# A decoder layer on one core: rsqrt on VectorE, a home for wo's last weights, queries stored in reading order, a third output tile

## Chip, cores and metric

The kernel runs on one core of one Trainium2 chip. The metric is the device time of one execution in microseconds (us). The core has five engines that run side by side, each through its own instructions in order: TensorE (PE, matmuls and transposes), VectorE (DVE), ScalarE (ACT), GpSimd (POOL) and SyncE (SP, which here issues nearly all DMAs).

## The reference, cut to what matters

```python
def hybrid_mixer(u, pos, w_in, g_cq, g_ckv, w_uq, w_uk, w_uv, w_iq, w_up_a, w_up_b, w_o):
    ...
    o_a = dsa_branch(c_q, c_kv, k_rope, k_idx, w_idx, pos, w_uq, w_uk, w_uv, w_iq)
    o_b = dilated_branch(qkv_b.reshape(B, S, 3, N_GROUPS_B, H_B, D_HEAD_B), pos)
    g_a, g_b = jnp.split(gates, 2, axis=-1)
    z = jax.nn.sigmoid(g_a) * (o_a @ w_up_a) + jax.nn.sigmoid(g_b) * (o_b @ w_up_b)
    return z @ w_o

def reference(x, c, positions, ...):
    ...
    h = rms_norm(x, g_pre_ffn1) * (1 + sc1) + sh1
    x = x + 0.5 * gt1 * rms_norm(swiglu(h, w_gate1, w_up1, w_down1), g_post_ffn1)
    u = rms_norm(x, g_pre_mix) * (1 + sc2) + sh2
    y = hybrid_mixer(u, positions, ...)
    x = x + gt2 * rms_norm(y, g_post_mix)
    h = rms_norm(x, g_pre_ffn2) * (1 + sc3) + sh3
    return x + 0.5 * gt3 * rms_norm(swiglu(h, w_gate2, w_up2, w_down2), g_post_ffn2)
```

There are 1024 tokens, a model width of 1024 and a hidden width of 2816, all in float32. Branch A is a sparse attention: each token's index scores choose 256 earlier keys (top-k), and eight heads attend to these. Branch B is a dilated sliding window with three groups (g = 0, 1, 2) of four heads.

## The kernel before

A float32 matmul is made of three passes over operands that are split into a high and a low part (`mm3`, lines 104 to 106; the split is a copy on ACT, L76, and a subtraction on DVE, L77, or on POOL, L82). The tokens are eight tiles t of 128. The order in which instructions stand on each engine is set when the program is built, by a scheduler that lists what is ready by its own cost estimates; tile pools with a fixed number of buffers are part of what it looks at. On the chip every engine then runs its list in order and waits on semaphores.

In time the program goes: modulation and the first feed-forward (to about 757 us), `mixer_front` (the projections of u, the index scores and branch A's queries), `branch_b`, `branch_a`, `mixer_out`, the output projection `wo`, and the second feed-forward (FFN2).

**Queries.** `mixer_front` makes branch A's queries for one token tile at a time as a high part `qh` and a low part `ql` of 128 x 8 x 128 numbers, and stores each in DRAM as one block of `qd` (L823, L824). `branch_a` works on head pairs p. Its `queries(p)` (L1158) loads the two heads of a pair, high and low, for all eight tiles into `QQ` (the trace's `aq`): four DMAs of 512 KB each per pair, sixteen in all.

**Branch B.** For each group there are eight steps T of 128 queries. A step projects q, k (`bq`) and, for g = 0, v (`bv`); DVE applies the rotation (L994, L996); PE transposes to `bqT`, `KH` and `KL` (L1015); PE makes scores `bs` for two heads (L1033, L1034); DVE adds the mask and takes the maximum (L1037, which also writes columns of `ob`); ACT exponentiates (L1042); PE transposes (`bpt`, L1048) and multiplies with the values `bV` (L1056, L1059); ACT and DVE put the result in `ob` (L1063, L1064); and SP stores `ob` to `bd` (L1069). The tile `ob` has two buffers. For g = 1 and 2 the values are loaded from `vd` (L988). The first group's weights come in through raw buffers `wbr` (L944) of the pool `r3`, three of them. The gates' projections `gpj`, whose weights `gr` are loaded on L903, and the top-k's counting rounds on DVE (L849) run at the same time as the first group.

**Branch A's start.** It loads keys `KK`, `Ke`, `Ko` (L1119) and the queries, makes `kpj`, then scores `as`. Later `combine_b` reads `bd` back (`br`, L1076).

**wo.** The loop is over two halves h of four token tiles and two column halves c. One set of weights (one h, one c) is eight row blocks of 128 x 512, each with a high tile (`woh`) and a low tile (`wol`), in a pool `w3` of thirteen buffers. For each of the four token tiles j, `wo` is summed over eight k, three passes each. After both column halves, `residual` and `prenorm` follow for each tile. Each contains one `rsqrt`: eight small instructions on numbers of 128 x 1 (L88, L89, then three rounds of L94 and L95), and L1292 ahead of the first. They run on POOL, except the residual of t = 4, 6 and the prenorm of t = 5, 7, which run on DVE. The large steps L1294 (residual) and L1302 (prenorm) are on DVE. `xt` holds the residual stream of a half; the first half's is in the tile `gab`, the second half's in the third buffer of the tag `z`, whose first two hold `mixer_out`'s result.

**FFN2's start.** `first_half` turns (L208, L214) and splits the first half's normed rows to the operands V[0] and V[1]; `second_half` needs the second half's rows too and makes differences of the two (L232 on DVE) for V[2] to V[6]. `gate_up` prepares combined weights on POOL (L286 to L289) and runs the matmuls `gu`; DVE and POOL combine what comes out (L372, L380).

Of the kernel before, what the change touches and what calls it, by code (L numbers as in the profile page):

```python
# [10 lines left out]
F32 = mybir.dt.float32  # L11
F32R = mybir.dt.float32r
# [8 lines left out]
D = 1024  # L21
S = 1024
DFF = 2816
P = 128
# [11 lines left out]
def f(t):  # L36
    return t.bitcast(F32)


class Layer:  # L40
# [581 lines left out]
        nc.vector.tensor_tensor(out1, out1, t[0], op=ALU.subtract)  # L622
        nc.vector.tensor_tensor(out2, out2, t[1], op=ALU.add)

    def load_w(self, W, src, n, name, rows=1024, per=None, split=None, rawp=None):

        nc = self.nc
        per = per or 1024 // n
        his, los = [], []
        nk = rows // P  # L630
        for k0 in range(0, nk, per):
            m = min(per, nk - k0)
            r = (rawp or self.rawp).tile([P, m, n], F32, name=f"{name}r", tag="raw")
            nc.sync.dma_start(r, src[k0 * P:(k0 + m) * P, :].rearrange("(k p) f -> p k f", p=P))
            for j in range(m):
                hi = W.tile([P, n], F32R, name=f"{name}h", tag="w")
                lo = W.tile([P, n], F32R, name=f"{name}l", tag="w")
                (split or self.split)(hi, lo, r[:, j, :])
                his.append(hi)
                los.append(lo)  # L640
        return his, los

    def mixer_front(self, uT, second, W, cp, ce, mk, tb):
# [150 lines left out]
        for t in range(8):  # L794
# [22 lines left out]
            for g in range(2):  # L817
                bt = self.bank("qtr")
                for j in range(4):
                    nc.tensor.transpose(bt[:, j * P:(j + 1) * P], qt[:, 4 * g + j, :], self.ident)  # L820
                self.split(qh[:, 4 * g:4 * g + 4, :].rearrange("p a b -> p (a b)"),
                           ql[:, 4 * g:4 * g + 4, :].rearrange("p a b -> p (a b)"), bt)
            nc.sync.dma_start(self.qd[0, t], f(qh))  # L823
            nc.sync.dma_start(self.qd[1, t], f(ql))  # L824
        return sc, gp, idxp

    def topk(self, sc, pool, mask, off, bp):
# [85 lines left out]
    def branch_b(self, uT, W, bp, last, gates, raws):  # L913
# [9 lines left out]
        for g in (0, None, 1, 2):  # L923
# [37 lines left out]
            for T in range(8):  # L961
# [61 lines left out]
                else:  # L1023
                    blocks, lo_c, kk = [(0, V), (1, prev)], 0, lambda x: x[:, 0::2, :]
                Pm = [bp.tile([P, 2, 256], F32, name="bP", tag="bP", bufs=2) for _ in range(2)]
                ob = bp.tile([P, 264], F32, name="ob", bufs=2)
                mask = self.wide[g // 2][:, P:] if prev is not None and slot == 0 else self.wide[g // 2]
                for hp in range(2):
                    bs = self.bank("bs", tag="s")
# [69 lines left out]
    def branch_a(self, aw, ap, late, G, mask, off):  # L1099
# [55 lines left out]
        def queries(p):  # L1155
            for e in range(2):
                for l in range(2):
                    nc.sync.dma_start(f(QQ[:, e, l]), self.qd[l, :, :, 2 * p + e, :].rearrange("t p q -> p t q"))  # L1158

        keys(0)  # L1160
        queries(0)
# [145 lines left out]
def layer_kernel(ctx, tc, aps, out):  # L1307
    nc = tc.nc
# [108 lines left out]
    with pool("mk") as mk:  # L1417
        mask = mk.tile([P, o], BF, name="mask")
        L.turns = {}
        with pool("cp") as cp, pool("wa", 16) as W, pool("ce") as ce, pool("r2", 4) as L.rawp, pool("tb") as tb:  # L1420
            def second():
                L.emit_hT(uT, 1, [y1[:, j, :] for j in range(4)], sh2)
                right.close()
                ixp = ix.enter_context(pool("ix", side="right"))
                return right.enter_context(pool("gp", side="right")), ixp

            sc, gp, ixp = L.mixer_front(uT, second, W, cp, ce, mk, tb)
        with pool("wb", 24) as W, pool("bp") as bp, pool("r3", 3) as L.rawp:
            def raws():
                right.close()  # L1430
                return right.enter_context(pool("r7", 3, side="right"))

            L.branch_b(uT, W, bp, lambda: L.topk(sc, ixp, mask, off, bp), lambda: L.gates(uT, gp), raws)
            L.turns = {}
        right.close()
        ix.close()
        gq = right.enter_context(pool("gq", side="right"))
        G = gq.tile([P, 4096], F32R, name="gbuf")
        with pool("r4", 2, side="right") as L.rawp, pool("aw", side="right") as aw, pool("ap") as ap, pool("al") as late:
            oA, oB, wa0 = L.branch_a(aw, ap, late, G, mask, off)  # L1440
# [3 lines left out]
    with pool("w3", 13) as W, pool("r5", 3) as L.rawp, pool("o2") as op:  # L1444
# [5 lines left out]
        with pool("zp") as zp:  # L1450
# [6 lines left out]
            ss = sums()  # L1457
            for h in range(2):
                ys[h] = L.big.tile([P, 4, D], F32, name=f"wy{h}", tag="big")
                xt = zp.tile([P, 4, D], F32, name=f"xt{h}", **(dict(tag="z", bufs=3) if h else dict(tag="gab")))  # L1460
                nc.sync.dma_start(xt, L.x1[4 * h * P:(4 * h + 4) * P, :].rearrange("(t p) d -> p t d", p=P))
                for c in range(2):
                    cl = slice(c * 512, (c + 1) * 512)
                    wh, wl = L.load_w(W, aps["w_o"][0][:, cl], 512, "wo")
                    for j in range(4):
                        b = L.bank("wo", tag="pj")
                        for k in range(8):
                            L.mm3(b, z[h][0][:, k, tok(j)], z[h][1][:, k, tok(j)], wh[k], wl[k], k == 0, k == 7)
                        L.evac(jk, b, ys[h][:, j, cl], G[:, cl], ss[4 * h + j][:, c:c + 1])
                for j in range(4):  # L1470
                    t = 4 * h + j
                    L.residual(ys[h][:, j, :], xt[:, j, :], ss[t], ss[t][:, 2:3], nc.vector if t in (4, 6) else nc.gpsimd)
                    nc.sync.dma_start(x2[tok(t), :], xt[:, j, :])
                    L.prenorm(ys[h][:, j, :], xt[:, j, :], None, ss[t][:, 2:3], ss[t][:, 3:4], nc.vector if t in (5, 7) else nc.gpsimd)
                if h == 0:
                    V[0], V[1] = bigv(0), bigv(1)
                    L.first_half(V, ys[0], range(8), sh, a3)
# [69 lines left out]
```

## Time and profile before

| | before |
|---|---|
| median of 3 runs | 2488.96 us (2488.2 to 2491.31) |
| profiled execution, its own time | 2492.64 us |
| span of that execution in the trace | 2490.9 us |
| mean granted TensorE clock, as a share of full speed | 0.971 |
| PE busy | 2333.2 us (94%) |
| DVE busy | 1664.0 us (67%) |
| ACT busy | 1091.1 us (44%) |
| POOL busy | 1002.8 us (40%) |
| mean rate of the DMA queues | 132 GB/s |

Times in rows are us from the start of the span. A busy PE is one whose matmuls run or stand in the pipeline. Where a row says that an engine was idle "<-X", X is the instruction that released it by the trace. A granted clock of 1.00 is 2.4 GHz, and 0.50 is 1.2 GHz.

### The profile page before, as it was taken

How to read it: one execution, taken by the hardware profiler on the slowest of the kernel's cores; microseconds unless marked ns; L12 is line 12 of the kernel's file. 1: busy time of each engine (PE TensorE's matmuls, PEld its weight loads, DVE VectorE, ACT ScalarE, POOL GpSimd, SP SyncE). 2: the span in 40 equal slices, each digit the busy share in tenths (PEclk: the TensorE clock that was granted, in tenths of full speed). 3: DMA queues.
4: the chain of work that ended last, by engine and by line, in shares of the span. 5: the costliest groups of instructions: out<-in, count | busy, mean ns of one | idle time of the engine just before them, and what ended most of it. 6: DMA issues, size and time to landing. Idle time of an engine off the chain costs nothing.

```text
span 2490.9 us, 33864 instructions
## 1 busy us (share of the span) xinstructions
PE 2333.2 (94%) x11211; PEld 1956.6 (79%) x11211; DVE 1664.0 (67%) x3236; ACT 1091.1 (44%) x2346; POOL 1002.8 (40%) x1122
## 2 busy tenths in 40 slices
PE   5799999989998999999989799889889999999997
PEld 4588877778887977888989688768667888887876
DVE  7865779753886135899973378864477656555786
ACT  5432223323454345677635567632453333233443
POOL 5675555400004433242244200300488756652533
PEclk9899999999999999999999899999989999999999
DMA  9334554671543233521422422143343333336755
GB/s 280 92 103 127 150 156 147 222 268 51 182 137 107 78 100 99 177 63 35 131 85 59 108 69 69 52 169 127 127 135 117 126 108 111 94 123 232 245 194 203
DMA packets 244171, 327.55 MB, mean 132 GB/s; under 512 B 24535, under 2 KB 145271, under 8 KB 243997
## 3 DMA queue, kind: packets, MB, share of 16 engines
q1 hardware_dynamic: 243356, 324.33, 40.8%
q8 instruction: 89, 1.46, 0.2%
q10 hardware_dynamic: 640, 1.07, 0.1%
q14 instruction: 86, 0.70, 0.1%
HBM read 252.07 MB, written 73.27 MB: 131 GB/s over the span
## 4 chain that ended last, share of the span: by engine, by line
PE 69%; DVE 14%; DMA 7%; issue 4%; POOL 4%; ACT 3%; SPq 0%; DVEq 0%; POOLq 0%; ACTq 0%
PE gu L105 9%; PE gu L104 9%; PE gu L106 9%; PE dn L106 4%; PE dn L105 4%; PE dn L104 4%; PE gpj L104 2%; DMA wr<-in_w_mod_dram 2%; PE gpj L105 2%; PE gpj L106 2%; PE bq L104 2%; PE bq L105 2%; PE bq L106 1%; DMA re<-in_w_down_dram 1%; DVE wl L77 1%
## 5 line engine op out<-in xcount | busy, mean ns | idle before, releaser
L104 PE MATMUL gu<-V,wh 128*128 128x512 f32 x1232 | 489.6, 398 | 17.2 <-ACT wh L76 9.3
L105 PE MATMUL gu<-V,wl 128*128 128x512 f32 x1232 | 488.9, 397 | 6.6 <-DVE wl L77 5.7
L106 PE MATMUL gu<-V,wh 128*128 128x512 f32 x1232 | 484.3, 396 | 4.5 <-DVE V L77 4.5
L77 DVE TENSOR_TENSOR wl<-rw,wh 128x512 fp32r<-128x512 f32 x232 | 218.2, 943 | 111.3 <-PE gu L105 80.1
L104 PEld LDWEIGHTS gu<-V,wh 128*128 128x128 f32 x1232 | 235.4, 191 | 71.5 <-ACT wh L76 9.8
L105 PEld LDWEIGHTS gu<-V,wl 128*128 128x128 f32 x1232 | 235.0, 191 | 62.0 <-DVE wl L77 10.4
L106 PEld LDWEIGHTS gu<-V,wh 128*128 128x128 f32 x1232 | 234.6, 191 | 57.2 <-DVE V L77 7.7
L105 PE MATMUL dn<-dh,al 128*128 128x512 f32 x660 | 256.9, 392 | 0.2 <-DVE al L77 0.2
L106 PE MATMUL dn<-dl,ah 128*128 128x512 f32 x660 | 255.2, 392 | 1.1 <-DVE dl L77 1.0
L104 PE MATMUL dn<-dh,ah 128*128 128x512 f32 x660 | 239.0, 392 | 9.1 <-DVE junk L197 6.4
L76 ACT CAST wh<-rw 128x512 fp32r<-128x512 f32 x232 | 139.9, 618 | 213.1 <-PE gu L106 127.7
L372 DVE TENSOR_TENSOR p<-gu,p 128x512 f32<-128x512 f32 x252 | 169.8, 681 | 67.0 <-PE gu L106 33.6
L380 POOL TENSOR_TENSOR p<-p 128x512 f32<-128x512 f32 x86 | 132.1, 1537 | 202.9 <-DVE p L372 73.1
L104 PEld LDWEIGHTS dn<-dh,ah 128*128 128x128 f32 x660 | 124.3, 189 | 35.9 <-DVE junk L197 6.8
L378 ACT ACTIVATE p<-p 128x512 f32<-128x512 f32 x86 | 54.4, 633 | 222.2 <-DVE p L372 173.1
L106 PEld LDWEIGHTS dn<-dl,ah 128*128 128x128 f32 x660 | 124.6, 189 | 28.4 <-DVE dl L77 2.7
L105 PEld LDWEIGHTS dn<-dh,al 128*128 128x128 f32 x660 | 124.5, 189 | 27.3 <-DVE al L77 1.3
L185 DVE SCALAR_TENSOR_TENSOR macc<-wr,scol,macc 128x512 f32<-128x512 f32 x98 | 94.3, 962 | 52.7 <-DMA wr<-in_w_mod_dram 52.0
L76 ACT CAST dh<-rd 128x512 fp32r<-128x512 f32 x110 | 67.9, 619 | 117.5 <-PE dn L105 75.6
L77 DVE TENSOR_TENSOR dl<-rd,dh 128x512 fp32r<-128x512 f32 x110 | 77.1, 704 | 52.2 <-ACT dh L76 48.9
L104 PE MATMUL gpj<-uh,gw 128*128 128x512 f32 x256 | 103.8, 406 | 7.5 <-ACT gt L910 7.3
L849 DVE TENSOR_SCALAR_CACHE_REDUCE mask<-isc,cand 128x384 bf16<-128x384 f32 (+1 forms) x124 | 108.7, 877 | 2.6
(479 smaller groups left out, 5610.7 us busy)
## 6 DMA issues: line engine op xcount, KB each, us to landing
act<-p SPq DMA_DIRECT2D x122, 256.0 KB
rd<-in_w_down_dram SPq DMA_DIRECT2D x58, 512.0 KB
wr<-in_w_mod_dram SPq DMA_DIRECT2D x112, 256.0 KB
rw<-in_w_gate_dram SPq DMA_DIRECT2D x44, 512.0 KB
rw<-in_w_up_dram SPq DMA_DIRECT2D x44, 512.0 KB
ra<-act SPq DMA_DIRECT2D x35, 512.0 KB
act<-act SPq DMA_DIRECT2D x44, 256.0 KB
re<-in_w_down_dram SPq DMA_DIRECT2D x20, 512.0 KB
```

The costliest lines, as they stand in the source:

```text
L76: self.nc.scalar.copy(hi, src)
L77: self.nc.vector.tensor_sub(lo, src, f(hi))
L104: mm(out, ah, bh, start=start, stop=False)
L105: mm(out, al, bh, start=False, stop=False)
L106: mm(out, ah, bl, start=False, stop=stop)
L185: nc.vector.scalar_tensor_tensor(acc, r, self.scol[:, k:k + 1], acc, op0=ALU.mult, op1=ALU.add)
L372: nc.vector.tensor_tensor(x[m], bk, y[m], op=ALU.add)
L378: nc.scalar.activation(x[0], x[0], AF.Silu)
L380: nc.gpsimd.tensor_tensor(x[1], x[1], x[0], op=ALU.mult)
L849: nc.vector.tensor_scalar(mask[:, :(t + 1) * P], sc[t], 0.0 if v is None else one(f(v), t), 0.0, op0=op, op1=ALU.add, accum_out=one(cnt, t))
```

## The change

There are five edits.

1. In `wo`, all `rsqrt` chains and L1292 of `residual` and `prenorm` run on DVE.
2. The last set of `wo` (h = 1, c = 1) keeps its eight high tiles in one tile `wohi` in the third buffer of the tag `z`; only its eight low tiles use the pool `w3`. `xt` of the second half is now in `gab`, after the first half's.
3. `qd` is laid out in the order in which `branch_a` reads it. A store now writes 1024 pieces of 512 B in place of 128 of 4 KB, and a load reads 128 pieces of 4 KB in place of 1024 of 512 B.
4. `ob` has three buffers.
5. The raw pool `r3` of branch B has two buffers.

```diff
@@ load_w
-    def load_w(self, W, src, n, name, rows=1024, per=None, split=None, rawp=None):
+    def load_w(self, W, src, n, name, rows=1024, per=None, split=None, rawp=None, hi=None):
...
-        per = per or 1024 // n
+        per, room = per or 1024 // n, hi
...
-                hi = W.tile([P, n], F32R, name=f"{name}h", tag="w")
+                hi = W.tile([P, n], F32R, name=f"{name}h", tag="w") if room is None else room[:, k0 + j]
@@ mixer_front
-            nc.sync.dma_start(self.qd[0, t], f(qh))
-            nc.sync.dma_start(self.qd[1, t], f(ql))
+            for l, x in enumerate((qh, ql)):
+                nc.sync.dma_start(self.qd[l, :, :, t, :].rearrange("e p q -> p e q"), f(x))
@@ branch_b
-                ob = bp.tile([P, 264], F32, name="ob", bufs=2)
+                ob = bp.tile([P, 264], F32, name="ob", bufs=3)
@@ branch_a, queries
-                    nc.sync.dma_start(f(QQ[:, e, l]), self.qd[l, :, :, 2 * p + e, :].rearrange("t p q -> p t q"))
+                    nc.sync.dma_start(f(QQ[:, e, l]), self.qd[l, 2 * p + e])
@@ the stage of branch B
-        with pool("wb", 24) as W, pool("bp") as bp, pool("r3", 3) as L.rawp:
+        with pool("wb", 24) as W, pool("bp") as bp, pool("r3", 2) as L.rawp:
@@ wo
-                xt = zp.tile([P, 4, D], F32, name=f"xt{h}", **(dict(tag="z", bufs=3) if h else dict(tag="gab")))
+                xt = zp.tile([P, 4, D], F32, name=f"xt{h}", tag="gab")
...
-                    wh, wl = L.load_w(W, aps["w_o"][0][:, cl], 512, "wo")
+                    room = zp.tile([P, 8, 512], F32R, name="wohi", tag="z", bufs=3) if h and c else None
+                    wh, wl = L.load_w(W, aps["w_o"][0][:, cl], 512, "wo", hi=room)
...
-                    L.residual(ys[h][:, j, :], xt[:, j, :], ss[t], ss[t][:, 2:3], nc.vector if t in (4, 6) else nc.gpsimd)
+                    L.residual(ys[h][:, j, :], xt[:, j, :], ss[t], ss[t][:, 2:3], nc.vector)
...
-                    L.prenorm(ys[h][:, j, :], xt[:, j, :], None, ss[t][:, 2:3], ss[t][:, 3:4], nc.vector if t in (5, 7) else nc.gpsimd)
+                    L.prenorm(ys[h][:, j, :], xt[:, j, :], None, ss[t][:, 2:3], ss[t][:, 3:4], nc.vector)
```

The edits move instructions, since the scheduler lists anew. Three places show it.

SP's queue at the end of branch B's last group (T = 0 to 7 of g = 2), where A's keys (`KK`, `Ke`, `Ko`) and queries (`aq`) are loaded among B's stores (`bd<-ob`). Before:

```order
L1069 DMA bd<-ob 128x264
L977 DMA bcs<-csd 128x96
L1119 DMA KK<-krd 64x2x1024 x2
L1158 DMA aq<-qd 128x8x128 x4
L1119 DMA Ke_13582<-krd 64x2x1024
L1119 DMA Ko_13583<-krd 64x2x1024
L988 DMA bV<-vd 128x512 x2
L1069 DMA bd<-ob 128x264 x2
```

And after:

```order
L1119 DMA KK<-krd 64x2x1024 x2
L1158 DMA aq<-qd 128x1024
L977 DMA bcs<-csd 128x96
L988 DMA bV<-vd 128x512 x2
L1069 DMA bd<-ob 128x264
L1158 DMA aq<-qd 128x1024 x3
L1119 DMA Ke_13582<-krd 64x2x1024
L1069 DMA bd<-ob 128x264
L1119 DMA Ko_13583<-krd 64x2x1024
L988 DMA bV<-vd 128x512 x2
L1069 DMA bd<-ob 128x264 x2
```

T=0's store stands ahead of the keys in both. Before, the stores of T=1 and T=2 stood together behind all four query loads; now T=1's stands behind one of them, and T=2's behind the other three and `Ke`.

DVE at the end of `wo`, second half: L398 takes a finished block of `wo` out of PSUM, then the norm of a token tile follows. Before, behind the third and fourth block:

```order
L398 TENSOR_TENSOR wy_16989<-wo,G_16505 128x512
L1292 TENSOR_TENSOR sums<-sums 128x1
L94 TENSOR_SCALAR rs_t<-rs_y,rs_v 128x1
L77 TENSOR_TENSOR wl_17580<-re_17577,wh_17579 128x512
L398 TENSOR_TENSOR wy_16989<-wo,G_16505 128x512
L88 TENSOR_SCALAR rs_v<-sums 128x1
L95 TENSOR_SCALAR rs_y<-rs_t,rs_y 128x1
L89 TENSOR_SCALAR rs_y<-rs_v 128x1
L94 TENSOR_SCALAR rs_t<-rs_y,rs_v 128x1 x2
L95 TENSOR_SCALAR sums<-rs_t,rs_y 128x1
L1294 SCALAR_TENSOR_TENSOR xt_16990<-wy_16989,sums,xt_16990 128x1024
```

After, behind the second block:

```order
L95 TENSOR_SCALAR sums<-rs_t,rs_y 128x1 x2
L1294 SCALAR_TENSOR_TENSOR xt_16990<-wy_16989,sums,xt_16990 128x1024
L1302 TENSOR_SCALAR wy_16989<-xt_16990,sums 128x1024
L398 TENSOR_TENSOR wy_16989<-wo,G_16505 128x512
L1292 TENSOR_TENSOR sums<-sums 128x1
L77 TENSOR_TENSOR wl_17520<-re_17517,wh_17519 128x512
L88 TENSOR_SCALAR rs_v<-sums 128x1 x2
L89 TENSOR_SCALAR rs_y<-rs_v 128x1 x2
L77 TENSOR_TENSOR wl_17526<-re_17523,wh_17525 128x512
L94 TENSOR_SCALAR rs_t<-rs_y,rs_v 128x1 x2
```

Before, the first residual L1294 came after all four evacuations; now a tile's L1294 and the one before's L1302 stand between two evacuations, and a residual's and a prenorm's chains alternate (x2). On PE the last set's matmuls run as four blocks of 24, one token tile after the other, where before each token tile had 18 of them in a first round and its last six (two of the eight k) in a second.

DVE at the start of branch B's first group, where the top-k's counting rounds (L849) stand around the first step's rotation (L994, L996; `bV` is that step's values). Before:

```order
L849 TENSOR_SCALAR mask,cnt<-isc_7463,cand 128x384
L849 TENSOR_SCALAR mask,cnt<-isc_7532,cand 128x512
L849 TENSOR_SCALAR mask,cnt<-isc_7702,cand 128x768
L994 TENSOR_TENSOR qk<-bq,bcs 128x512
L996 TENSOR_TENSOR brt<-bq,bcs 128x512
L866 TENSOR_TENSOR need<-cnt,thr 128x2
L849 TENSOR_SCALAR mask,cnt<-isc_7803,cand 128x896
L77 TENSOR_TENSOR bV<-bv,bV 128x4x64
```

After:

```order
L866 TENSOR_TENSOR need<-cnt,thr 128x2
L849 TENSOR_SCALAR mask,cnt<-isc_7803,cand 128x896
L867 TENSOR_SCALAR acc<-need 128x2
L863 TENSOR_SCALAR acc<-cnt 128x4
L994 TENSOR_TENSOR qk<-bq,bcs 128x512
L996 TENSOR_TENSOR brt<-bq,bcs 128x512
L868 TENSOR_TENSOR pb<-pb,acc 128x2
L864 TENSOR_TENSOR pb<-pb,acc 128x4
L858 TENSOR_SCALAR cand<-pb 128x2
L77 TENSOR_TENSOR bV<-bv,bV 128x4x64
```

In the whole list, 37 of the L849 stood ahead of the first L994, and now 46. PE's gate matmuls `gpj` ahead of the second step's `bq` are 740 of 768, where they were 693.

## Rows read from the trace of the kernel before

**Rows 1.** The page, busy us, share of the span and instructions of each engine

```profile
PE 2333.2 (94%) x11211; PEld 1956.6 (79%) x11211; DVE 1664.0 (67%) x3236; ACT 1091.1 (44%) x2346; POOL 1002.8 (40%) x1122
```

**Rows 2.** Stretches: length; PE, PEld, DVE, ACT, POOL busy (instructions); PE clock; DMA share; GB/s

```profile
1100.00:1250.00 150.00, 149.95 (x878) 138.99 (x876) 142.08 (x447) 102.20 (x239) 38.52 (x43) 1.00 0.26 79
...
1395.40:1451.70 56.30, 38.97 (x229) 33.74 (x227) 20.49 (x65) 28.76 (x83) 8.06 (x9) 0.73 0.38 94
...
1404.60:1421.70 17.10, 7.92 (x39) 7.11 (x39) 4.99 (x20) 6.88 (x22) 4.62 (x5) 0.50 0.37 86
```

**Rows 3.** Chain of waits, end of branch B: start, us, what

```profile
1403.04 10.20 DMA bd<-ob
1413.38 0.42 DVE bP L1037
...
1424.27 2.81 DMA bd<-ob
1427.22 0.43 DVE bP L1037
...
1437.85 2.13 DMA bd<-ob
```

**Rows 4.** SyncE's DMA queue there: start, us, engine, line, what, count

```profile
1390.03 9.32 SPq L1158 DMA_DIRECT2D aq<-qd  x4
...
1403.04 0.86 SPq L1069 DMA_DIRECT2D bd<-ob  x2
```

**Rows 5.** VectorE, end of wo: start, us, instruction, [idle before it <- releaser]

```profile
1779.05 0.75 DVE L1302 TENSOR_SCALAR wy<-xt,sums 128x1024 f32<-128x1024 f32 x1 [0.45 <-POOL sums L95]
...
1804.50 0.69 DVE L77 TENSOR_TENSOR wol<-wor,woh 128x512 fp32r<-128x512 f32 x1 [11.06 <-PE wo L105]
...
1840.31 0.76 DVE L1302 TENSOR_SCALAR wy<-xt,sums 128x1024 f32<-128x1024 f32 x1
...
1843.18 0.95 DVE L232 TENSOR_TENSOR wy<-wy,wy 128x512 f32<-128x512 f32 x1 [1.51 <-ACT wy L216]
```

**Rows 6.** Stretches behind wo's last matmul, columns as in rows 2

```profile
1811.80:1843.20 31.40, 28.94 (x124) 23.27 (x123) 22.53 (x56) 17.55 (x34) 24.51 (x41) 0.95 0.67 217
1843.20:1884.60 41.40, 31.00 (x104) 21.68 (x102) 35.84 (x34) 18.03 (x31) 37.48 (x23) 0.73 0.15 45
1855.20:1872.30 17.10, 13.29 (x34) 9.22 (x35) 17.10 (x18) 9.89 (x18) 13.82 (x9) 0.50 0.25 70
1879.00:1885.80 6.80, 5.89 (x13) 3.68 (x14) 5.59 (x6) 1.24 (x2) 6.17 (x5) 0.50 0.06 9
```

**Rows 7.** VectorE, end of branch B, columns as in rows 5

```profile
1398.62 0.42 DVE L1064 TENSOR_TENSOR ob<-bo,ob 128x256 f32<-128x256 f32 x1 [3.44 <-ACT ob L1063]
```

**Rows 8.** DMA rate in 40 slices, of 1391 to 1399.5 and of 992.6 to 1056 us

```profile
GB/s 366 405 308 289 270 135 212 270 96 251 270 231 135 289 251 135 231 231 96 200 200 193 171 164 224 292 296 299 299 297 296 299 282 296 289 289 292 287 289 292
...
GB/s 206 403 62 10 165 0 0 225 331 194 122 43 0 207 406 293 14 0 10 251 406 5 0 184 395 248 0 85 81 163 406 176 189 237 241 362 254 39 343 277
```

**Rows 9.** Line L94, the whole span: ns min/median/max, first and last start

```profile
L94 DVE TENSOR_SCALAR rs_t<-rs_y,rs_v x63: 253/266/274, 697.6 to 2485.2; 128x1 f32<-128x1 f32 x63
L94 POOL TENSOR_SCALAR rs_t<-rs_y,rs_v x57: 334/341/1820, 1751.5 to 2482.9; 128x1 f32<-128x1 f32 x57
```

**Rows 10.** POOL's groups, 1749 to 1779 us: count | busy us, mean ns | idle before

```profile
L94 POOL TENSOR_SCALAR rs_t<-rs_y,rs_v 128x1 f32<-128x1 f32 x24 | 11.1, 470 | 0.8
```

**Rows 11.** The page's costliest groups, columns as in rows 10

```profile
L849 DVE TENSOR_SCALAR_CACHE_REDUCE mask<-isc,cand 128x384 bf16<-128x384 f32 (+1 forms) x124 | 108.7, 877 | 2.6
```

**Rows 12.** PE's waits, 1030 to 1300 us: us in total, times, longest

```profile
PE bq L104 <- DVE brt L996: 6.5, 3, 3.2
```

**Rows 13.** VectorE's groups, 1843 to 1885 us, columns as in rows 10

```profile
L232 DVE TENSOR_TENSOR wy<-wy,wy 128x512 f32<-128x512 f32 x8 | 10.3, 1285 | 2.7 <-ACT wy L216 1.5 <-POOL V L82 1.2
```

**Rows 14.** VectorE, second half's operands, columns as in rows 5

```profile
1868.03 0.68 DVE L232 TENSOR_TENSOR wy<-wy 128x512 f32<-128x512 f32 x1
...
1875.43 1.76 DVE L232 TENSOR_TENSOR wy<-wy,wy 128x512 f32<-128x512 f32 x1 [1.19 <-POOL V L82]
```

## The prediction

> **What bounds the kernel now.** The page's first line is read first: TensorE (PE) is busy 94% of the span [rows 1]. An edit therefore pays only where PE stands still or has been granted the low clock. The table of stretches says where: from 1100 to 1250 us, with branch B's first group, the gates and the top-k side by side, PE is busy 149.95 of 150 us at clock 1.00, with VectorE (DVE) at 142 [rows 2]. Two other stretches have room, and the change touches both.
>
> The first is the end of branch B's last group. From 1395.4 to 1451.7 us PE works 38.97 of 56.3 us at a mean clock of 0.73 [rows 2]. The chain of waits names the cause [rows 3]: three pieces "DMA bd<-ob" of 10.20, 2.81 and 2.13 us, each ending in DVE's L1037. A step T may write its `ob` only when the store of step T-2 has landed. The store of T=1 is late because of SyncE's queue [rows 4]: the four loads of A's queries hold SP for 9.32 us from 1390.03, and the two `bd` stores behind them leave at 1403.04.
>
> The second is the end of `w_o` and the start of the second feed-forward (FFN2). The last `wo` matmul ends at about 1811.8. DVE stands idle 11.06 us before 1804.50, since the last weight tiles have no slot until PE frees one; the last prenorm L1302 starts at 1840.31, and the second half of V's operands (L232) at 1843.18 [rows 5]. From there to 1884.6 PE works 31.0 of 41.4 us at a mean clock of 0.73, beside a DVE that is busy 35.84 and a GpSimd (POOL) that is busy 37.48 [rows 6].
>
> **Part 1: three ob tiles.** With three tiles, step T waits for the store of T-3. T=3, the one that waited 10.20 us, now waits for T=0's store, which stands ahead of the query loads in SP's order. Its L1037 could go as soon as PE's scores are there, about 1402, not at 1413.38: 11.4 us. T=5 and T=7 then need the stores of T=2 and T=4. In the changed order T=2's store stands behind three query loads and the `Ke` load, 2 MB. At the 297 GB/s that the late slices of the load stretch show [rows 8] they take 7 us; they follow T=1's store, whose `ob` is finished at 1399 [rows 7], so T=2's store lands near 1410 with its own 2 to 3 us. T=5 followed T=3 by 13.84 us before [rows 3], of which 2.81 are a store's wait; so 11 us, and T=5 stands at about 1413, behind that landing. Its wait falls away, and T=7's 2.13 with it: 15.1 us for the three pieces. On top comes clock: PE ran at 0.50 from 1404.6 to 1421.7, with 7.92 us busy [rows 2]; at the full level half of that, 4 us, would go, and I take 3. Sum **-18**. Ends: the whole idle time, 17.3, plus 4 is the most, -21; if T=5 waits for T=2's store as long as T=3 does now, little more than the two small pieces is left, -5.
>
> **Part 2: wo's last set and its norms.** Before, the sixteen tiles of the last set have thirteen slots, so PE runs all four row blocks on six of the eight k first, and every block ends in the last 7 us. With the eight high tiles in `room` the blocks run one after the other: DVE's order now has an evacuation, a norm, an evacuation, a norm. The norms of t=4 to 6 then lie beside the remaining blocks, and only t=7's is left behind the last matmul. Its chain on DVE is the evacuation 0.69, two rsqrt chains of eight small ops (about 1.7 us each, with L94 at 266 ns the longest of them [rows 9]), L1294 1.3 to 2.3 and L1302 0.75: some 8 us with ScalarE's square, and about 14 with the L77 and L372 that stand between. So the last L1302 moves from 28.5 us behind the last `wo` matmul to 14. As DVE sets the pace of the 41.4 us that follow (35.84 busy), what it starts 14 to 16 us earlier ends so much earlier; PE meanwhile has 144 `gu` matmuls that need none of it, 34 us at the 28.94 us for 124 instructions of [rows 6], and transposes. I take -16. The most is what PE could get back from 1811.8 to 1884.6: idle 2.5 and 10.4, and half of the 13.29 and 5.89 us that it works at 0.50 [rows 6], 9.6; together -22. The least, -4, is under the second rival.
>
> The first half's norms (t=0 to 3) now run on DVE too. POOL's 24 L94 took 470 ns each there [rows 10], against DVE's 266 [rows 9]. But DVE must also split some nine weight tiles in that place, and its own sum (eight chains of 1.7, four L1294 of 1.2, four L1302 of 0.7, the splits) is some 28 us from 1750, where the last of these L1302 starts at 1779.05 before [rows 5]. So -2, between 0 and -5. The whole of part 2: **-18**.
>
> POOL's L94 takes 341 ns as a median of all its places [rows 9], and 470 in this one, beside DVE's L1294 [rows 10]. The Trainium skill, "SBUF — State Buffer", section "SBUF: two separate sides", says that VectorE with two SBUF inputs and GpSimd lock each other out for a whole instruction. The rows agree; by it the moved chains lose the stretch, while the L232 that follow stay exposed to POOL.
>
> **Part 3: the queries in DRAM.** The 16 stores of 512 KB now go out in 512 B pieces, and the 16 loads come in whole 4 KB rows. The stores' stretch reaches 406 GB/s in single slices, the loads' 297 [rows 8]. At these, 8.4 MB cost 20.7 or 28.2 us of queue time: +7.5 us, spread over the 64 us in which the stores go out, with idle slices between, so it is hidden unless a `wbr` or `gr` load behind a store is late. Four loads cost 7.1 us before and 5.2 now; in branch A they are hidden save for the `br` reads behind them: -1, between 0 and -3.
>
> The Trainium skill, "DMA: Bandwidth & Descriptors", section "Specifications", gives 512 B as the size from which a transfer runs at line rate. By that neither direction changes, part 3 is 0, and the sum is a microsecond smaller. The rows speak against it (297 against 406 GB/s), though one is a read and the other a write.
>
> **Part 4: B's raw buffers, three to two.** The first group's weights now have two raw tiles. In the changed order nine more of the top-k's counts stand ahead of step T=0's L994; at 877 ns [rows 11] that is 7.9 us. The gates' matmuls move ahead to fill PE, so nothing is lost at once; but they are used up by T=3 rather than T=7, and PE then hangs on DVE, which has 8 us to spare in 150 [rows 2]. Before, PE waits 6.5 us for L996 from 1030 to 1300 [rows 12]. So 0 to +8; I take **+2**, since DVE's work is the same in sum.
>
> **The sum.** -18 - 18 - 1 + 2 = -35. The profiled execution took 2492.64 us: 2457.6. The median, 2488.96, is 3.7 below it, so the forecast is **2454**. By the ends it is 2489 - 21 - 27 - 3 = 2438 to 2489 - 5 - 4 + 8 = 2488.
>
> **Rivals.** First, in B the wait only changes its name: `bV` of T=5 and T=6 and T=2's store all stand behind the query loads, and if those run late T=5 waits as T=3 did. Part 1 gives -6: 2466. For it: SP's queue is the cause now, and one more tile doesn't shorten it. Against: T=5 needs its store 11 us after T=3 starts, and the loads take 7.
>
> Second, FFN2's start is paced by DVE and POOL together. L232 takes a mean of 1285 ns there [rows 13], 0.68 us at the least and 1.76 beside POOL [rows 14]. If the operands come sooner but meet POOL every time, some 24 such ops (L232, V's and the weights' L77) cost 0.5 us more each, 12 us, and part 2 is -6: 2466. The load of `xt` for the second half, now in the tile that the first half frees, can be late in the same place and has the same price. For it: POOL is 91% busy there. Against: the same DVE ops stand beside the same POOL work as before. The first page named above states the lock that would do this.
>
> Third, slower: the first group starves. With two raw tiles each `wbr` load waits for a split that stands behind the top-k in its engine's order, and SP, which issues in order, holds the gates' loads and the 512 B stores back meanwhile. PE then has neither gates nor queries. It decides from 35 us of new PE idle time on; with six counts more of waiting ahead of each of the eight steps, 8 x 6 x 0.877 = 42 us, and 4 us of stores in front, it gives 2500. Against: PE has no idle time in 150 us, and the gates are filler that was moved ahead.
>
> Fourth, the change doesn't do what it says: the stores in B are late for another reason, and the norms wait for the last weights as before. Then only parts 3 and 4 remain: 2490, within 0.2%.
>
> **Chances.** Forecast (2442 to 2462) 0.56; first rival 0.14; second 0.18; third 0.06; fourth 0.06. The range that leaves at most two in ten out reaches from 2438, the sum of the best ends, to 2473, where one part fails in full and the first group costs its 8. A measurement of this kernel can tell 0.2%, 5 us, from no change. Faster 0.88, the same 0.06, slower 0.06.
>
> **What would show it.** In the changed profile the chain in B has no "bd<-ob" piece over 3 us, and the stretch from the query loads to A's first `kpj` is 18 us shorter. From the end of `wo` the last prenorm is about 14 us away, and PE's low clock behind it is gone or short. POOL shows no rsqrt ops in `wo`. The prediction is wrong if L1037 of T=5 waits as T=3 did, if PE stands idle behind `wo` as long as before, or if PE waits over 15 us in all between 1050 and 1300.

## The result and the profile after

| | before | changed |
|---|---|---|
| median | 2488.58 us (2484.29 to 2491.31, 4 runs) | 2470.53 us (2467.49 to 2472.95, 4 runs) |
| ratio to before, 95% interval | | 0.9921 [0.9905, 0.9937] |
| profiled execution; its span | 2492.64; 2490.9 us | 2467.49; 2465.7 us |
| mean granted clock | 0.971 | 0.978 |

The change gains 18 us, where 35 were forecast. The two profiled executions lie 25 us apart, of which 5 arose before the first instruction that the change touches.

To see where the time went, PE's matmuls are counted: every kernel of this study has 11211. Parts of branch B and of `wo` come in another order in some kernels, but at each border below all of them have run the same matmuls, so the start of the n-th can be set against the start of the n-th of before. The table shows what each stage added (+) or saved (-) against the one trace of before, in us. "First" is matmuls 4500 to 6104 (branch B's first group and most of the second), "B's end" 6104 to 6750 (the rest of B and branch A's start), "A" 6750 to 8000 (branch A and the merge), "wo" 8000 to 8750 (from wo to steady FFN2). The stage ahead, of which the change touches only the stores of the queries, shows how far two executions drift. The expectations below count the first stage to matmul 6250, where the kernels with edit 5 still owe 18 of the projections `bq` that before has run; by that border 3 us less are lost and 3 us less are gained (+9.5 and -13.0 for the changed kernel).

Where PE's time is split below, "idle" is time in which PE has no matmul, and "work at 0.50" is time in which it works at the low level, half of which is lost.

| kernel | ahead | first | B's end | A | wo | whole trace |
|---|---|---|---|---|---|---|
| changed | -5.0 | +12.6 | -16.2 | -3.0 | -13.7 | -25.5 |
| changed, once more (e12) | +1.3 | +11.8 | -15.6 | -2.8 | -13.4 | -19.1 |
| e1: two raw buffers | -0.7 | +12.6 | -7.2 | -2.3 | +2.4 | +4.2 |
| e2: queries' layout | +3.1 | -0.3 | -0.3 | -4.0 | +0.1 | -2.1 |
| e3: third ob, two raw buffers | -1.1 | +11.2 | -12.2 | +0.6 | +1.4 | -1.8 |
| e4: both wo edits | -3.7 | +0.4 | +4.8 | -4.3 | -14.3 | -17.1 |
| e5: rsqrt on DVE | -1.5 | +0.4 | +4.8 | -2.1 | -9.2 | -8.7 |
| e6: room for the weights | -3.2 | +0.3 | +5.2 | -3.9 | -8.4 | -10.6 |
| e7: small tile for statistics | -2.2 | -1.8 | -11.1 | -0.6 | -0.8 | -16.9 |
| e8: small tile, queries, wo | -1.2 | +0.6 | -9.9 | -2.7 | -13.2 | -27.4 |
| e11: e8 once more | -2.2 | -1.1 | -11.0 | -3.9 | -14.2 | -31.9 |
| e9: query loads by ACT | -3.4 | +0.1 | +0.8 | -0.5 | 0.0 | -4.2 |
| e10: e8 and query loads by ACT | -2.6 | +0.7 | -13.6 | -2.9 | -13.9 | -32.8 |

Both traces of the changed kernel say the same of each stage within 1 us: a loss of about 12 in the first stage, gains of about 16 in B's end and 13.5 around `wo`, some 3 in between.

**B's first group.** The stretch from 1120 to 1260 us of the changed kernel (columns as in [rows 2]), and PE's waits from 1100 to 1260:

```profile
1120.00:1260.00 140.00, 133.99 (x747) 124.21 (x745) 129.49 (x373) 86.70 (x199) 34.41 (x34) 0.95 0.26 80
```

```profile
PE bo L1056 <- ACT bPT L76: 1.9, 3, 1.2
PE bo L1059 <- DVE bPT L77: 1.5, 2, 1.2
PE bq L104 <- DVE bV L77: 0.9, 1, 0.9
```

Where PE was busy without a break [rows 2], it now stands 6 of 140 us, in waits of 1.2 us and less, and the clock falls to 0.50 twice behind them:

```profile
1183.00:1189.00 6.00, 5.70 (x27) 5.41 (x27) 6.00 (x13) 4.56 (x14) 2.98 (x4) 0.50 0.38 95
1203.20:1209.80 6.60, 6.60 (x24) 5.91 (x25) 6.46 (x22) 4.26 (x11) 0.00 (x0) 0.50 0.28 102
```

The 6 us of idle time and half of these 12.6 us make 12.3, near the table's 12.6. All of the loss lies in the first group: at matmul 5514, which stands at 1230 us in the trace of before, the changed kernel has lost 13.4 us. From 1050 to 1300 us, the stretch that the prediction named, PE stands 16.0 us (15.3 in e12), where it stood 9.9:

```profile
1050.00:1300.00 250.00, 234.04 (x1239) 210.00 (x1238) 223.46 (x616) 148.08 (x354) 84.97 (x105) 0.96 0.28 85
```

**B's end.** No "bd<-ob" stands in the chain any more [rows 3]. What stands there is the rotation of the next step, which goes to and fro between POOL and DVE through tiles of one buffer (chain of waits, columns as in [rows 3]):

```profile
1403.95 1.30 POOL bkl L82
1405.27 0.69 DVE qk L994
1405.96 0.61 DVE brt L996
1406.75 0.66 issue
1407.41 0.73 POOL qk L1002
1408.14 1.04 issue
1409.21 0.73 POOL bqn L82
1409.95 1.25 POOL bkl L82
```

The stretch, and its part at low clock:

```profile
1397.00:1443.60 46.60, 42.19 (x242) 36.87 (x242) 20.59 (x65) 27.71 (x79) 9.83 (x12) 0.82 0.50 142
1418.20:1435.30 17.10, 15.53 (x65) 13.05 (x64) 5.69 (x22) 8.72 (x28) 0.15 (x1) 0.50 0.11 31
```

PE stands 4.4 us here, not the 17.3 of [rows 2]; but 17.1 us still run at the low level. Over the stage, idle time falls from 18.7 to 4.8 us and work at 0.50 from 19.6 to 15.5: 13.9 and half of 4.1 make the 16. SP's queue (as [rows 4]) has the order that the program's list promised, T=1's store behind one query load:

```profile
1396.47 1.28 SPq L1158 DMA_DIRECT2D aq<-qd  x1
...
1399.28 0.37 SPq L1069 DMA_DIRECT2D bd<-ob  x1
1399.99 3.76 SPq L1158 DMA_DIRECT2D aq<-qd  x3
1407.12 0.58 SPq L1119 DMA_DIRECT2D Ke<-krd  x1
1407.80 0.54 SPq L1069 DMA_DIRECT2D bd<-ob  x1
```

**wo and FFN2's start.** From the first to the last `wo` matmul it takes 102.1 us, where it was 105.8, and PE works 94.92 of these (before, then changed):

```profile
1706.00:1811.80 105.80, 95.93 (x417) 76.92 (x416) 44.12 (x63) 37.92 (x76) 33.65 (x74) 0.95 0.41 137
1694.50:1796.60 102.10, 94.92 (x418) 76.99 (x417) 64.14 (x181) 42.45 (x87) 9.64 (x7) 0.97 0.45 156
```

DVE there (as [rows 5]): the last prenorm stands 12.6 us behind the end of `wo`, not 28.5, and the first L232 19.0, not 31.4.

```profile
1809.18 1.82 DVE L1302 TENSOR_SCALAR wy<-xt,sums 128x1024 f32<-128x1024 f32 x1
...
1815.57 0.69 DVE L232 TENSOR_TENSOR wy<-wy,wy 128x512 f32<-128x512 f32 x1 [1.20 <-ACT wy L216]
```

And yet PE is steady only at about 1861, 64.4 us behind `wo`, where it was about 73. Its longest pause is no longer one for V but for a weight (PE's timeline), whose sums POOL makes (POOL's timeline):

```profile
1837.98 1.31 PE L104 MATMUL gu<-V,wh 128*128 128x512 f32 x2 [5.00 <-ACT wh L76]
```

```profile
1822.91 1.30 POOL L286 TENSOR_TENSOR s<-rw,rw 128x512 f32<-128x512 f32 x1
1824.17 1.75 POOL L287 TENSOR_TENSOR rw<-rw 128x512 f32<-128x512 f32 x1
1825.87 1.74 POOL L380 TENSOR_TENSOR p<-p 128x512 f32<-128x512 f32 x1
1827.57 1.74 POOL L232 TENSOR_TENSOR wy<-wy,wy 128x512 f32<-128x512 f32 x1
1829.27 1.75 POOL L287 TENSOR_TENSOR rw<-rw 128x512 f32<-128x512 f32 x1
1830.97 1.74 POOL L82 TENSOR_TENSOR V<-wy,V 128x512 fp32r<-128x512 f32 x1
1832.67 1.26 POOL L288 TENSOR_TENSOR rw<-s,rw 128x512 f32<-128x512 f32 x1
```

The stretch of the second half's operands (as [rows 6]) is 45.4 us long, where it was 41.4, with POOL busy 38.41 and DVE 41.81:

```profile
1815.60:1861.00 45.40, 34.36 (x141) 25.76 (x140) 41.81 (x38) 21.29 (x37) 38.41 (x25) 0.89 0.25 78
```

What PE got back behind `wo` is mostly clock. From the last `wo` matmul to the steady state it stands 11.0 us, where it stood 12.9 [rows 6]; its work at 0.50 falls from 22.5 us to 7.4, in one stretch of 10.2:

```profile
1838.00:1848.20 10.20, 7.36 (x15) 4.53 (x16) 10.20 (x9) 4.81 (x9) 10.20 (x7) 0.50 0.00 0
1796.40:1861.00 64.60, 53.56 (x229) 41.48 (x229) 56.93 (x75) 33.01 (x57) 43.62 (x29) 0.92 0.37 114
```

### The profile page after: what moved, and what is told of

It is laid out like the page before. It is cut to its first block, busy times and chain, and to the rows that moved or that the text cites. A ratio compares the mean times of both kernels' runs of the same rounds, so it can differ in the third digit from the quotient of the medians.

```text
span 2465.7 us, 33880 instructions
## 1 busy us (share of the span) xinstructions
PE 2325.7 (94%) x11211; PEld 1954.8 (79%) x11211; DVE 1687.8 (68%) x3338; ACT 1091.0 (44%) x2346; POOL 964.5 (39%) x1020
## 3 DMA queue, kind: packets, MB, share of 16 engines
q1 hardware_dynamic: 243356, 324.33, 41.4%
## 4 chain that ended last, share of the span: by engine, by line
PE 70%; DVE 13%; DMA 6%; issue 4%; ACT 4%; POOL 2%; SPq 0%; DVEq 0%; POOLq 0%; ACTq 0%
PE gu L104 10%; PE gu L105 9%; PE gu L106 9%; PE dn L105 4%; PE dn L104 4%; PE dn L106 4%; PE gpj L104 2%; PE gpj L105 2%; PE gpj L106 2%; PE bq L104 2%; DMA wr<-in_w_mod_dram 2%; PE bq L105 2%; PE bq L106 2%; PE apv L1220 1%; DVE al L77 1%
## 5 line engine op out<-in xcount | busy, mean ns | idle before, releaser
L77 DVE TENSOR_TENSOR wl<-rw,wh 128x512 fp32r<-128x512 f32 x232 | 224.5, 971 | 106.6 <-PE gu L105 79.6
L104 PEld LDWEIGHTS gu<-V,wh 128*128 128x128 f32 x1232 | 234.0, 190 | 78.9 <-ACT wh L76 17.6
L849 DVE TENSOR_SCALAR_CACHE_REDUCE mask<-isc,cand 128x384 bf16<-128x384 f32 (+1 forms) x124 | 108.8, 877 | 2.8
L77 DVE TENSOR_TENSOR dl<-rd,dh 128x512 fp32r<-128x512 f32 x110 | 78.8, 719 | 46.4 <-ACT dh L76 43.0
```

The source lines that it names most:

```text
L77: self.nc.vector.tensor_sub(lo, src, f(hi))
L104: mm(out, ah, bh, start=start, stop=False)
L849: nc.vector.tensor_scalar(mask[:, :(t + 1) * P], sc[t], 0.0 if v is None else one(f(v), t), 0.0, op0=op, op1=ALU.add, accum_out=one(cnt, t))
```

## Experiments

Each edit's diff is against the kernel before unless said. Ratios are to runs of before on the same chip; medians differ between chips, so ratios and the table of stages are compared.

**e1: two raw buffers alone.**

```diff
-pool("r3", 3) as L.rawp
+pool("r3", 2) as L.rawp
```

> The kernel before with edit 5 alone: branch B's raw pool has two buffers, not three. Theory (the two raw buffers cost the first group its time): DVE's and PE's orders in the first group become those of the changed kernel, PE gains small gaps and low clock there between 1120 and 1310 us, and the run is 9 to 10 us slower than before, near 2498. Rival (the 512 B stores of the queries cost it): this run is within 2 us of before.

2497.54 us, ratio 1.0015 [1.0002, 1.0027]: slower by 4 us, not by 9. The stages say why: the first group loses 12.6 us, as in the changed kernel and with the same waits, and B's end gives back 7.2. PE's wait for L1037 in B's end (waits, 1395 to 1456: in total, times, longest), whose longest was 8.85 us before, is now

```profile
PE bs L1033 <- DVE ob L1037: 2.7, 2, 1.4
```

with two `ob` tiles still: in this order, too, T=1's store leaves behind one query load, not four. PE's idle time in B's end falls from 18.7 us to 7.5, but its work at 0.50 grows from 19.6 us to 27.3. So edit 5 carries the loss, and by its order of the queue most of the idle time that was put down to edit 4. Edit 5 lets the gates run out sooner and gives DVE another order; no run does one of these without the other.

**e2: the queries' layout alone** (edit 3 of the change, as its diff shows it).

> The kernel before with edit 3 alone: queries stored in reading order. The order of every engine's compute instructions is that of before. Theory (raw buffers): within 2 us of before, near 2488, with branch A 1 us shorter. Rival (512 B stores): 8 to 10 us slower, lost between 990 and 1310 us, near 2497.

2488.99 us, ratio 0.9986 [0.9972, 1.0001]. The first group is as before: the 512 B stores are hidden, and the rival falls. In branch A the six traces with this layout save 2.7 to 4.0 us, the others between +0.6 and -4.3, in the mean 1.3 less; that is no more than the drift.

In B's end, e2 shows what holds T=1's store. The four loads now keep SP for 1.96 us, not 9.32 [rows 4], and the store leaves at 1401.85, right behind the instruction that finishes its `ob` (DVE's L1064, to 1401.82). In the chain it takes longer than before's 10.20 us [rows 3] all the same; the second row is how busy the DMA engines are, in tenths, in 40 slices from 1393 to 1414 us:

```profile
1401.85 11.91 DMA bd<-ob
DMA  0699899979799999999998999999999999810000
```

The engines are busy until about 1411 us, and the wait for the store ends shortly behind that. So T=1's store is late here for the loads that it finds in the DMA engines, not for a hold of SP. PE's idle time in B's end is still 4.0 us shorter here (14.7 for 18.7), but its work at 0.50 is 8.3 us longer, which takes the gain back.

**e3: third ob tile and two raw buffers** (edits 4 and 5).

> The kernel before with edits 4 and 5: three ob tiles, two raw buffers (three and three don't fit). Theory: the end of branch B gains 13 us as in the changed kernel, and the first group loses 9 to 10, so about 3 to 4 us faster than before, near 2485. Rival (the gain in B's end came from the queries' faster loads, not from the tile): the end of B gains 5 us or less and the run is 4 us or more slower than before.

2490.53 us, ratio 0.9993 [0.998, 1.0007]. No difference from before is shown by the times. B's end gains 12.2 us and the first group loses 11.2. Over e1 the tile itself saves 5.0 in B's end; the changed kernel saves 3 to 4 more with the same order of stores. The queue shows one difference, the three query loads ahead of T=2's store, which hold SP for 6.69 us here against 3.76:

```profile
1402.50 6.69 SPq L1158 DMA_DIRECT2D aq<-qd  x3
...
1411.02 0.54 SPq L1069 DMA_DIRECT2D bd<-ob  x1
```

So the rival may be right in part, the faster loads having a share in B's end; alone (e2) they shorten the idle time there. But the low clock also lasted 23.9 us in B's end here, and 17.1 and 20.5 in the two traces of the changed kernel: of their 4.0 and 3.4 us over e3, 1.0 and 1.9 are idle time and 3.4 and 1.7 the clock. Whether the loads brought the clock back sooner stays open.

**e4: both wo edits; e5: rsqrt on DVE alone; e6: room for the weights alone** (edits 1 and 2).

> The kernel before with edits 1 and 2 alone: wo's norms on DVE and room for the last weights. Theory: the stretch from the first wo matmul to steady FFN2 is 13 to 14 us shorter, near 2475, which is faster than the whole change measured minus its loss in the first group. Rival (part of that gain in the changed kernel hangs on branch A ending sooner): 8 us or less, near 2481.

2478.76 us, ratio 0.9942 [0.9927, 0.9957]. The stage saves 14.3 us, as in the changed kernel: it hangs on nothing ahead of it.

> The kernel before with edit 1 alone: all rsqrt chains of wo's norms on DVE; the last set of weights still waits for slots. Theory (the room for the weights carries the gain, since it lets three norms lie beside matmuls): 3 to 5 us of the 14 from wo's start to steady FFN2. Rival (POOL's slow chains carry it): 9 us or more.

2483.78 us, ratio 0.9954 [0.9938, 0.9971]; 9.2 us in the stage, so the theory (3 to 5) falls and the rival (9 or more) holds. Most of it lies within `wo`, from the first matmul to the last 99.3 us instead of 105.8:

```profile
1707.60:1806.90 99.30, 95.08 (x417) 77.32 (x416) 52.23 (x131) 38.77 (x76) 7.65 (x6) 0.97 0.43 146
```

The chains of t = 0 to 3 on POOL had held the transposes there for longer than the sum of DVE's work had let expect: PE's waits for L1302 and L214 between 1700 and 1815 us were 9.2 us, and are 2.1.

> The kernel before with edit 2 alone: room for wo's last high tiles, rsqrt chains on POOL and DVE as before. Theory: 9 to 11 us of the 14, and low clock behind wo for 17 us or less, where it was 27.3 us. Rival: 4 us or less, since the POOL chains stay behind the last matmul.

2481.96 us, ratio 0.9959 [0.9939, 0.9979]; 8.4 us in the stage, a little under the 9 to 11 expected, all behind the last `wo` matmul (from the first to the last it takes 105.6). The last prenorm stands 17 us behind it, with chains on POOL. Alone, the two save 9.2 and 8.4; together 14.3, not 17.6. Of the 3.3 us between, 2 are lost within `wo`, which takes 101.1 us in e4 and 99.3 in e5, and 1 behind it. PE's pause for `wh`, behind POOL's sums, is there in e4 (5.24), e6 (4.36) and the changed kernel (5.00); the longest of e5, 4.46, is for the transposes, behind DVE's L214. Why the two edits don't add is not shown, and 3.3 us is not much more than the drift of this stage, which is 2.4 us longer in e1, where no edit touches it.

**e7: a small tile for the statistics.** It cures the wait at its root, since L1037 and the exponentials write only eight columns of `ob`, and takes 96 bytes per partition, where the third `ob` takes 1056 and doesn't fit beside three raw buffers.

```diff
                 ob = bp.tile([P, 264], F32, name="ob", bufs=2)
+                st8 = bp.tile([P, 8], F32, name="ost", bufs=3)
...
-                accum_out=ob[:, 260 + hd:261 + hd])
+                accum_out=st8[:, 4 + hd:5 + hd])
...
-                accum_out=ob[:, 256 + hd:257 + hd])
+                accum_out=st8[:, hd:hd + 1])
...
                 nc.vector.tensor_add(ov, bo4[:, :, 0, :], ov)
+                nc.scalar.copy(ob[:, 256:264], st8)
```

> The kernel before with another cure for the wait in B: the eight columns of maxima and sums that L1037 and the exponentials write get a small tile of three buffers, and ScalarE copies them into ob at the step's end; ob keeps two buffers and the raw pool three. Theory: the first group is as before within 2 us (three raw buffers), and the end of B gains 8 us or more of its idle time, near 2480. Rival (the gain in the changed kernel's B came from the order that two raw buffers gave): the end of B gains under 4 us.

2482.42 us, ratio 0.9955 [0.9934, 0.9976]. B's end gains 11.1 us with three raw buffers, and the first group loses nothing. The cure of the wait and the loss in the first group are separate things.

**e8: the changed kernel with e7's tile and three raw buffers** in place of edits 4 and 5.

> The changed kernel with the small tile for the maxima and sums in place of the third ob tile, and three raw buffers, which now fit. Theory: the first group's loss of 9 to 10 us is gone and the rest stays, so 27 to 30 us faster than before and 9 to 11 faster than the changed kernel. Rival (the parts don't add, as the end of B needs the order that two raw buffers gave): 4 us faster than the changed kernel or less.

2466.33 us, ratio 0.9884 [0.9861, 0.9906]. The first group is whole again, in the same stretch as above:

```profile
1120.00:1260.00 140.00, 139.91 (x782) 131.03 (x781) 132.72 (x389) 88.92 (x208) 38.70 (x40) 1.00 0.30 94
```

B's end saves 9.9, less than the changed kernel's 16: ScalarE's copy into `ob` now waits for a store (ScalarE's timeline), with the next `bPT` behind it, for which PE waits 5.2 us.

```profile
1405.27 0.20 ACT L1066 COPY ob<-ost 128x8 f32<-128x8 f32 x1 [4.78 <-DMA bd<-ob]
```

**e9: the query loads issued by ScalarE.**

```diff
-nc.sync.dma_start(f(QQ[:, e, l]), ...)
+(nc.sync if p else nc.scalar).dma_start(f(QQ[:, e, l]), ...)
```

> The kernel before with one edit that the change doesn't have: the four loads of A's first queries are issued by ScalarE, not SyncE, so B's stores don't stand behind them in SP's order; PE's and DVE's orders are those of before. Theory (SP's order holds the stores of T=1 and T=2): they leave some 9 us earlier, L1037 of T=3 waits under 4 us, and the end of B is 6 to 9 us shorter with two ob tiles, near 2481. Rival (the loads fill the DMA engines, whoever issues them, so the stores land as late): 3 us or less.

2489.41 us, ratio 0.9991 [0.9976, 1.0005]: nothing gained, since the edit made a wait of its own. ScalarE stands at its own loads (timeline):

```profile
1388.42 8.79 ACTq L1158 DMA_DIRECT2D aq<-qd  x2
1397.25 0.59 ACT L76 CAST bPT<-bpt 128x512 fp32r<-128x512 f32 x1 [9.19 <-issue]
```

T=1's `ob` is finished at 1402 rather than 1399 for that, its store leaves when it is ready, and takes 6.80 us in the chain. L1037 of T=3 waits 1.72 us, not 10.51, but the time is spent ahead of it. With e2, where the store also left at once and took 11.91 us, this speaks for the rival: the loads fill the DMA engines, whoever issues them.

**e10: e8 with that edit; e11 and e12: e8 and the changed kernel on the same chip.**

> Experiment e8_best with the four query loads on ScalarE's queue as well. Theory: the remaining gap of 5.2 us in B's end, where ScalarE's copy into ob waits for a store, shrinks, 3 to 5 us faster than e8_best. Rival (ScalarE is held by the loads that it issues, and exponentials wait behind them): no faster than e8_best.

2459.9 us, ratio 0.9869 [0.985, 0.9887].

> e8_best once more, beside the changed kernel on one chip. Theory: 5 to 6 us faster than the changed kernel, as the traces of both say: the first group's 10 us are back, and B's end gives up 4 of them. Rival: the two are alike within 2 us.

2462.67 us, ratio 0.9881 [0.9864, 0.9898].

> The changed kernel once more, for the comparison with e11_best on one chip: about 0.992 of before.

2466.95 us, ratio 0.9908 [0.9891, 0.9926]. By the medians e11 is 4.3 us faster than the changed kernel; the two intervals overlap by a little. By the stages of the two traces it is 13 us faster in the first group and gives 4.6 back in B's end. e10 saves 2.6 us more than e11 in B's end, but the intervals of the two cover each other, so that step isn't shown by the times. It is the fastest kernel here all the same, 7 us below the changed one by the medians, and its interval lies below that of the changed one.

## Why the prediction was half right

**The sign and the places were right.** The gains came from B's end and from wo to FFN2, and the queries' layout was worth 1 us or so. The size was half, -18 for -35, and two terms carry most of that: Part 4 was 10 us off, Part 2 some 4, Part 1 some 2. The median, 2470.53, lies inside the stated range, 2438 to 2473, but not for the reason given for its end ("one part fails in full and the first group costs its 8"): no part failed in full, and the first group cost 12.

**The prediction's own signs.** No piece "bd<-ob" stands in the chain, the last prenorm stands 12.6 us behind `wo`, the low clock behind it is 10.2 us where it was 27.3, and POOL runs no `rsqrt` there, as stated. But of the three signs of being wrong one came, PE's waits between 1050 and 1300 (15.7 us in all by the list of waits, over the 15 named; 9.8 before), and one nearly did: behind `wo` PE stands idle almost as long as before (11.0 us for 12.9).

**Part 4, +2, was +12 and the largest miss.** The step that failed is "PE then hangs on DVE, which has 8 us to spare in 150 ... since DVE's work is the same in sum". DVE's sum is the same; but small waits behind ACT and DVE, none over 1.2 us, came to the surface once the gates' matmuls were used up by T=3, 6 us in 140, and the clock fell behind them, some 13 us at half speed. The term's upper end, 8, took in DVE's delay and not the clock. e1 shows 12.6 from that edit alone. That the gates had filled these waits before is read from the orders and not shown by a run of its own. The third rival had the place right and the mechanism wrong: no wait of PE there names a load.

**Part 1, -18, was -16 against the trace of before: the size right, the cause in part not.** The idle time did go, 17.3 to 4.4, near the 15.1 of the three waits, and of the 3 us of clock some 2 came. How firm that is, e4 to e6 show: their order in B's end is the one of before and they need 5 us more there, mostly for low clock (below). Against their traces the change gains 21. The split of causes was off: in e1, with two `ob` tiles, the idle time is already 7.5 of 18.7 us, by the order of the queue that edit 5 brings; the third tile takes 1.7 more of it (e3: 5.8), and e3 leaves open what hangs on the faster loads. e7 shows that a tile alone, with three raw buffers, takes 7.5 of it. And "The store of T=1 is late because of SyncE's queue" named the smaller part: SP held the store for 4.0 us, from 1399.04 [rows 7] to 1403.04, and it then took 10.20 [rows 3]; e2, with SP free, shows the DMA engines full. The first rival (the wait goes to `bV` or T=2's store) didn't come true in the changed kernel; in e3 L1037 waits 2.03 us for T=2's store.

**Part 2, -18, was -13.6,** and its two halves were mis-sized both ways. The first half's norms were worth 3.7 in the changed kernel and 6.5 alone (e5), not 2. Behind the last matmul the prenorm moved as forecast (12.6 us for 14), and L232 with it by 12.4; but PE's gain there was 9.8, not 16, some 2 us of it idle time and 7.5 clock. The step that failed is "As DVE sets the pace of the 41.4 us that follow (35.84 busy), what it starts 14 to 16 us earlier ends so much earlier": the stretch began 12.4 us sooner and took 45.4. The next in line was POOL: its sums for the following weights take 1.3 to 1.75 us each and lie in one row with the operands' L82 and L232, and PE ran out of weights for 5.0 us before it needed V. That is the second rival by place, DVE and POOL together, at a third of its price: -13.6 lies between the -18 forecast and its -6. The Trainium skill's sentence that the port pair which the two share is an exclusive lock for a whole instruction ("SBUF — State Buffer", "SBUF: two separate sides") agrees with these rows: whichever starts first has it. POOL's L288 takes 1.26 us at 1832.67, just ahead of an L232 on DVE, and 1.71 at 1835.58, where an L77 on DVE is already running.

**Part 3** was right as far as it can be told: e2 shows no loss in the stores' stretch, and A's gain is within the drift. That 512 B rows load slower than 4 KB rows, which the prediction could only read from loads against stores, e2 shows with loads alone: in the last ten slices of the 8.5 us behind the first load they reach 308 to 463 GB/s, where before reads 282 to 299 in its last fifteen [rows 8]. The row of e2, 1392.8 to 1401.3 us:

```profile
GB/s 289 19 0 0 251 501 347 270 173 173 289 154 174 270 135 212 308 270 173 173 308 135 173 251 174 251 251 173 308 386 328 463 386 347 463 424 308 463 424 328
```

The difference is against the Trainium skill, which gives 512 B as the least size for line rate ("DMA: Bandwidth & Descriptors", "Specifications").

The sum by what was measured: -16 - 13.6 + 12 - 3 = -20.6, against -18 by the medians and 0.0092 x 2491, -23, in the second comparison.

## What to carry to other kernels

An engine that is busy without a break because of filler may hide small waits; an edit that uses the filler up sooner can cost these waits and the low clock behind them, so price it by the waits under the filler, not by the spare time of the engine beside it. When a store is late behind loads, ask whether it leaves late or lands late. When a tile's third buffer costs another pool its third, look which columns are waited for: eight columns in a tile of their own did nearly the same for a tenth of the room. Count idle time and work at the low clock apart: an edit can win one and lose the other (e1, e2). Where one stall goes, ask which engine's row stands next, and take its work, not that of the engine that waited last, as the new pace.

## What the runs showed of the hardware

The clock was less settled than the instruction order. In B's end, e4 to e6 and the kernel before have the same order on PE and 15 to 19 us of PE idle time, yet the low level lasted 30.7 us in the trace of before, 37.6 in e4 and e6, and 44.4 in e5, there without a break:

```profile
1404.30:1448.70 44.40, 31.88 (x139) 27.81 (x139) 13.42 (x53) 19.88 (x62) 5.37 (x6) 0.50 0.25 66
```

With idle times that differ from before's by 2.3 us or less, B's end took 5 us more in e4 to e6 than before, between kernels that don't differ there, and that is as large as several terms of the prediction. The stage ahead drifted too, between -5.0 and +3.1 us. A DMA that an engine issues for itself can hold that engine's arithmetic: 9.19 us on ScalarE (e9).
